# The first load of v: its second half as copies of 80, 44 and 4 rows

## The chip, the core and the metric

The kernel runs on one core of a Trainium2 chip. The time is the device time of one execution in microseconds (us); three executions before the change give the median used here. The profile is of one further execution, whose own time is told beside its span. The core has a matrix engine (PE, whose weight loads are shown as PEld), a vector engine (DVE), a scalar engine (ACT), GpSimd (POOL) and SyncE (SP), and 16 DMA engines that move data between HBM and the on-chip memory. Copies issued by SP go through the DMA queue that the profile calls q1, those issued by POOL through q0; POOL's can convert float32 to bfloat16 on the way.

## What is computed

Attention weights times values, for 8 batches and 12 heads:

```python
batch, n_heads, seq, head_dim = 8, 12, 1024, 64
np.einsum('bhqs,bhsd->bhqd', attn_weights, v).astype(np.float32)
```

`attn_weights` is float32 of 8 x 12 x 1024 x 1024 (403 MB), `v` and the result are float32 of 8 x 12 x 1024 x 64 (25 MB each).

## The kernel before, in words

**Tiling.** Four heads form a group q; there are 24 groups. Each of the 128 partitions holds 32 query rows of one head of the group. A group is worked on in two units of 16 rows each, so there are 48 units n. One load (`load_attn`, L316 to L322, issued by POOL) brings a unit into `abf[n % 2]`: 64 KB of float32 per partition, written as 32 KB of bfloat16. Two such buffers exist. The loads of the last two units are cut in halves.

**A unit.** PE transposes the 16 rows g of `abf` in groups of four matmuls (`transpose_g`, L127 to L140) into four banks; from g = 4 on, a group waits until the bank's earlier content has been copied out (L129). The copies into `at` are shared (`copy_g`, L254): DVE has ten of the sixteen rows (`on_dve`, L73), ACT six. In the first unit of each group PE also spreads v over the partitions (`spread_v`, L142) from `vr`, and DVE and ACT copy the result to `vbf`. Then PE transposes the last unit's output back (L156), multiplies (L169), and DVE and ACT copy the products to `ot`.

**v.** One load of v serves two groups (eight heads); `vr` has dimensions for the two. From the second load on, POOL loads v with conversion straight into `vr` (`load_v`, L324). The first load takes another way: SP copies it as float32 into `v32` (L383 to L387), which lies in two slots of the output buffer `osb` that are not used until late, and DVE casts it into `vr` (L308, L309). Per partition either half of v32 is 8 KB.

**Order.** Each engine has its own list of instructions, written out by hand, with semaphores between them. SP's list begins with the copies of v0, a release of output slots (L388) and a wait for the constants (L389), and goes on with one wait per load, which it passes on to PE (L390 to L410). DVE's begins with four memsets, the wait for v0 (L308) and the cast (L309); its copies of unit 0 come behind these. POOL's begins with loads 0 and 1, builds the constants, and then issues load n + 2 as soon as PE has done the transposes of unit n (L371, L372), with the loads of v and the stores of the output between them. The stores of the last eight groups are held back to the end.

**Fifteen little copies** (L397 to L402) are issued by SP beside unit 33. The k-th copies k + 1 elements of each of k partitions of the identity matrix; nothing reads them.

```python
        nc.vector.wait_ge(s_v0, 16 * 3)
        nc.vector.tensor_copy(out=vr.rearrange("p two b x -> p (two b x)"), in_=v32).then_inc(s_vr, 2)
        ...
        for two, p0, pn in ((0, 0, 16), (0, 16, P - 16), (1, 0, P)):
            nc.sync.dma_start(
                out=v32_2[ds(p0, pn), two], in_=v_2[0][ds(p0, pn), two]
            ).then_inc(s_v0, 16)
```

Of the kernel before, what the change touches and what calls it, by code (L numbers as in the profile page):

```python
# [10 lines left out]
def kernel(  # L11
# [18 lines left out]
    nc = tc.nc  # L30
# [7 lines left out]
    P = 128  # L38
# [44 lines left out]
    with tc.tile_critical(no_gpsimd_drain=True):  # L83
# [21 lines left out]
        s_v0, s_v = sem("s_v0"), sem("s_v")  # L105
# [199 lines left out]

        for h in range(2):
            nc.vector.memset(ot[:, :, ds(h * HP, HP)], 0.0).then_inc(s_ot[h])
        nc.vector.wait_ge(s_v0, 16 * 3)  # L308
        nc.vector.tensor_copy(out=vr.rearrange("p two b x -> p (two b x)"), in_=v32).then_inc(s_vr, 2)  # L309
        engine(True)  # L310
        engine(False)
# [69 lines left out]


        v32_2 = v32.rearrange("p (two x) -> p two x", two=2)  # L383
        for two, p0, pn in ((0, 0, 16), (0, 16, P - 16), (1, 0, P)):
            nc.sync.dma_start(
                out=v32_2[ds(p0, pn), two], in_=v_2[0][ds(p0, pn), two]
            ).then_inc(s_v0, 16)  # L387
# [68 lines left out]
```

## Time and profile before

| | |
|---|---|
| three executions | 1058.11, 1054.57, 1057.73 us |
| median | 1057.73 us |
| profiled execution, its own time | 1054.64 us |
| its span, first to last instruction | 1052.8 us |
| busy share of PE, DVE, ACT, POOL | 70%, 37%, 38%, 4% |
| copies of v0 by SP: 128 KB, 896 KB, 1024 KB | landed 2.9, 5.3, 26.5 us after issue |
| loads of a unit, median from issue to landing | 33.4 us |
| load 0 waited for by PE until | 28.21 us |
| v0 waited for by DVE until | 28.43 us |

Times inside the profiled execution are counted from the span's start. "Busy" of an engine leaves out its waits. In the profile's list of copies, the size is that of the written side, so a unit's load shows as 4096 KB though 8 MB are read. A line of the timeline gives start, duration, engine, source line, operation, destination and source, the number of instructions merged, and in brackets how long the engine had been idle and what ended that. A line of the DMA queues gives packets, megabytes, and the time the packets took as a share of the 16 engines' time. Besides the pages, the trace has a record of each packet's queue, start, duration and written size, and the times at which a copy's semaphore rose.

### The profile page before, as it was taken

How to read it: one execution, taken by the hardware profiler on the slowest of the kernel's cores; microseconds unless marked ns; L12 is line 12 of the kernel's file. 1: busy time of each engine (PE TensorE's matmuls, PEld its weight loads, DVE VectorE, ACT ScalarE, POOL GpSimd, SP SyncE). 2: the span in 40 equal slices, each digit the busy share in tenths (PEclk: the TensorE clock that was granted, in tenths of full speed). 3: DMA queues.
4: the chain of work that ended last, by engine and by line, in shares of the span. 5: the costliest groups of instructions: out<-in, count | busy, mean ns of one | idle time of the engine just before them, and what ended most of it. 6: DMA issues, size and time to landing. Idle time of an engine off the chain costs nothing.

```text
span 1052.8 us, 16298 instructions
## 1 busy us (share of the span) xinstructions
PE 734.0 (70%) x6920; PEld 688.6 (65%) x6920; DVE 388.4 (37%) x582; ACT 397.7 (38%) x485; POOL 45.0 (4%) x80
## 2 busy tenths in 40 slices
PE   0787687676687667667768667775666865975885
PEld 0776586566687567656668557765666865865875
DVE  0443344333353234333335324433333433532543
ACT  0443344433353334333335324433333533533543
POOL 1000000000000000000000000000000000000000
PEclk9989888898798888889879878888987987988998
DMA  9999999999999999999999999999999999999998
GB/s 234 223 218 218 205 256 219 219 216 248 229 214 256 210 218 258 219 219 230 242 218 209 258 218 219 259 218 218 249 214 219 217 212 227 219 206 226 210 215 341
DMA packets 14569, 240.21 MB, mean 228 GB/s; under 512 B 1506, under 2 KB 2018, under 8 KB 4962
## 3 DMA queue, kind: packets, MB, share of 16 engines
q0 software_dynamic: 12912, 233.84, 99.0%
q1 hardware_dynamic: 1650, 6.30, 1.6%
q8 instruction: 2, 0.03, 0.0%
q14 instruction: 5, 0.04, 0.0%
HBM read 427.82 MB, written 25.17 MB: 430 GB/s over the span
## 4 chain that ended last, share of the span: by engine, by line
DMA 78%; PE 21%; issue 1%; POOL 0%; DVE 0%; ACT 0%; POOLq 0%; SPq 0%
DMA abf<-in_attn_weights_dram 78%; PE bank L132 20%; PE bank L174 0%; PE bank L159 0%; POOL abf L319 0%; DVE osb L239 0%; ACT ot L268 0%; POOLq L451 0%; SPq L396 0%; SPq L83 0%
## 5 line engine op out<-in xcount | busy, mean ns | idle before, releaser
L132 PE MATMUL bank<-ident,abf 128*128 128x128 f32 x3072 | 450.1, 317 | 277.2 <-DMA abf<-in_attn_weights_dram 273.3
L132 PEld LDWEIGHTS bank<-ident,abf 128*128 128x128 f32 x3072 | 440.6, 214 | 290.1 <-DMA abf<-in_attn_weights_dram 285.4
L256 DVE COPY at<-bank 128x1024 bf16<-128x1024 bf16 x480 | 320.0, 689 | 468.4 <-PE bank L132 464.2
L256 ACT COPY at<-bank 128x1024 bf16<-128x1024 bf16 x288 | 288.7, 1012 | 430.2 <-PE bank L132 430.2
L174 PE MATMUL bank<-at,vbf 128*64 128x256 bf16 x3072 | 215.0, 278 | 0.0
L174 PEld LDWEIGHTS bank<-at,vbf 128*64 128x64 bf16 x3072 | 196.8, 108 | 13.4 <-DVE at L256 4.0
L268 ACT COPY ot<-bank 128x512 f32<-128x512 f32 x48 | 28.1, 586 | 181.0 <-PE bank L174 181.0
L268 DVE COPY ot<-bank 128x512 f32<-128x512 f32 x48 | 33.2, 692 | 151.4 <-PE bank L174 151.4
L159 PE MATMUL bank<-ident,ot 128*128 128x128 f32 x392 | 52.2, 276 | 32.9 <-DVE vbf L232 32.2
L159 PEld LDWEIGHTS bank<-ident,ot 128*128 128x128 f32 x392 | 43.4, 141 | 45.0 <-DVE vbf L232 44.0
L239 ACT COPY osb<-bank 128x512 f32<-128x512 f32 x97 | 52.2, 589 | 22.5 <-PE bank L159 22.5
L319 POOL DMA_DIRECT2D abf<-in_attn_weights_dram x50 | 27.2, 545 | 690.8 <-PE bank L132 689.8
L232 DVE CAST vbf<-bank 128x512 bf16<-128x512 f32 x48 | 30.9, 686 | 6.5 <-PE bank L147 6.5
L232 ACT CAST vbf<-bank 128x512 bf16<-128x512 f32 x48 | 25.8, 589 | 11.8 <-PE bank L147 11.8
L147 PE MATMUL bank<-vr,spread 32*128 32x512 bf16 x384 | 25.8, 377 | 0.0
L325 POOL DMA_DIRECT2D vr<-in_v_dram x11 | 7.7, 703 | 238.1 <-PE bank L147 238.1
L147 PEld LDWEIGHTS bank<-vr,spread 32*128 32x128 bf16 x384 | 10.1, 92 | 6.8
L309 DVE CAST vr<-osb 128x4096 bf16<-128x4096 f32 x1 | 2.3, 2294 | 25.9 <-DMA osb<-in_v_dram 25.9
L332 POOL DMA_DIRECT2D out_dram<-osb x10 | 7.1, 715 | 28.6 <-ACT osb L239 28.6
L256 ACT ACT_TABLE_LOAD x4 | 5.1, 1283 | 1.1 <-SPq L83 1.1
L356 POOL TENSOR_SCALAR_AFFINE_SELECT spread<-spread 32x512 bf16<-32x512 bf16 x4 | 2.5, 628 | 0.6
L239 DVE COPY osb<-bank 128x512 f32<-128x512 f32 x1 | 0.7, 692 | 3.1 <-PE bank L159 3.1
(8 smaller groups left out, 2.1 us busy)
## 6 DMA issues: line engine op xcount, KB each, us to landing
abf<-in_attn_weights_dram POOLq DMA_DIRECT2D x46, 4096.0 KB, 33.4
out_dram<-osb POOLq DMA_DIRECT2D x10, 2048.0 KB, 29.5
vr<-in_v_dram POOLq DMA_DIRECT2D x11, 1024.0 KB, 17.4
abf<-in_attn_weights_dram POOLq DMA_DIRECT2D x4, 2048.0 KB, 24.2
out_dram<-osb SPq DMA_DIRECT2D x1, 2048.0 KB, 13.6
osb<-in_v_dram SPq DMA_DIRECT2D x1, 1024.0 KB, 26.5
out_dram<-osb SPq DMA_DIRECT2D x1, 1024.0 KB, 15.8
osb<-in_v_dram SPq DMA_DIRECT2D x1, 896.0 KB, 5.3
```

The costliest lines, as they stand in the source:

```text
L132: last = pe.matmul(out=pt[g % 4][:, k], lhsT=words[:, k], rhs=ident, is_transpose=True, start=(k == 0), stop=(k == KW - 1),)
L147: last = pe.matmul(out=ps, lhsT=spread[rows, b], rhs=vr[rows, two, b], start=(b == 0), stop=(b == VB - 1),)
L159: last = pe.matmul(out=ps[:, ds(j * P, P)], lhsT=ot[:, j0 + j], rhs=ident, is_transpose=True, start=(j == 0), stop=(j == jn - 1),)
L174: last = pe.matmul(out=outs, lhsT=vbf[:, 2 * kw + par, h], rhs=at[:, ds(half * GH, GH), kw, ds(h * VP, VP), par], start=(n == 0), stop=(n ...
L232: copy(out=vbf[:, :, h], in_=ps.rearrange("p (k d) -> p k d", k=SB)).then_inc(s_vbf[e])
L239: return copy(out=rows.rearrange("p (half j) d -> p j half d", half=2)[:, ds(j0, jn)], in_=ps[:, ds(0, jn * P)].rearrange("p (j half d) -> ...
L256: ins = copy(out=at[:, g].rearrange("c k j two -> c (k j two)"), in_=bank[g % 4].bitcast(bf16),)
L268: copy(out=ot.rearrange("c j (h p) -> c h j p", h=VH)[:, ds(2 * e, 2)], in_=po[e].rearrange("c (h j p) -> c h j p", h=2, j=GH),).then_inc( ...
L319: pool.dma_start(out=abf[n % 2][:, ds(g0, gn)].rearrange("p g s -> p (g s)"), in_=attn_q[n // 2][:, ds((n % 2 * G + g0) * S, gn * S)],).th ...
L325: pool.dma_start(out=vr.rearrange("p two b x -> p two (b x)"), in_=v_2[iv]).then_inc(s_v, 16)
L332: eng.dma_start(out=out_2[q // 2] if fours == 2 else out_q[q], in_=at_slot if fours == 2 else at_slot[:, 0], **({"single_packet": True} if ...
L356: pool.affine_select(out=spread[ds(h * VP, VP)], in_=spread[ds(h * VP, VP)], compare_op=mybir.AluOpType.not_equal, fill=1.0, base=0, patte ...
```

## The change

The second half of v0 is no longer one copy of 128 partitions but three, of 80, 44 and 4 partitions, issued one behind the other by SP on the same queue and to the same places. Each adds 16 to the same semaphore when it has landed, so that DVE's wait before the cast goes from 3 x 16 to 5 x 16. The first half keeps its copies of 16 and 112 partitions. No other engine's list changes; SP's has two instructions more.

```diff
-        nc.vector.wait_ge(s_v0, 16 * 3)
+        nc.vector.wait_ge(s_v0, 16 * 5)
         nc.vector.tensor_copy(out=vr.rearrange("p two b x -> p (two b x)"), in_=v32).then_inc(s_vr, 2)
...
-        for two, p0, pn in ((0, 0, 16), (0, 16, P - 16), (1, 0, P)):
+        for two, p0, pn in ((0, 0, 16), (0, 16, P - 16), (1, 0, 80), (1, 80, 44), (1, 124, 4)):
             nc.sync.dma_start(
                 out=v32_2[ds(p0, pn), two], in_=v_2[0][ds(p0, pn), two]
             ).then_inc(s_v0, 16)
```

## The prediction

> **What bounds the kernel now.** I read the page's totals first, then the chain that ended last, then the timeline of the first 60 us, and last the DMA view of one short window.
>
> ```profile
> span 1052.8 us, 16298 instructions
> DMA  9999999999999999999999999999999999999998
> q0 software_dynamic: 12912, 233.84, 99.0%
> q1 hardware_dynamic: 1650, 6.30, 1.6%
> HBM read 427.82 MB, written 25.17 MB: 430 GB/s over the span
> DMA abf<-in_attn_weights_dram 78%; PE bank L132 20%; PE bank L174 0%; PE bank L159 0%; POOL abf L319 0%; DVE osb L239 0%; ACT ot L268 0%; POOLq L451 0%; SPq L396 0%; SPq L83 0%
> osb<-in_v_dram SPq DMA_DIRECT2D x1, 1024.0 KB, 26.5
> ```
>
> The 16 DMA engines are at 9 in every slice but the last, and every other engine waits for them. So the end comes when the last DMA engine is through its bytes; what makes a DMA engine idle, or gives the last one more to do, costs its full length, and what PE, DVE or ACT do counts only if it delays the issue of a load. The last line quoted is the copy that is changed: the second half of v0 needs 26.5 us to land, the 896 KB copy ahead of it 5.3.
>
> ```profile
> 0.96 1.32 SPq L385 DMA_DIRECT2D osb<-in_v_dram  x3
> 1.48 1.24 POOL L319 DMA_DIRECT2D abf<-in_attn_weights_dram  x2 [1.04 <-SPq L83]
> 28.21 9.96 PE L132 MATMUL bank<-ident,abf 128*128 128x128 f32 x64 [28.21 <-DMA abf<-in_attn_weights_dram]
> 28.43 2.29 DVE L309 CAST vr<-osb 128x4096 bf16<-128x4096 f32 x1 [25.86 <-DMA osb<-in_v_dram]
> 30.64 1.28 DVE L256 COPY at<-bank 128x1024 bf16<-128x1024 bf16 x2
> 38.47 0.57 POOL L319 DMA_DIRECT2D abf<-in_attn_weights_dram  x1 [32.25 <-PE bank L132]
> 48.55 9.48 PE L132 MATMUL bank<-ident,abf 128*128 128x128 f32 x64 [2.54 <-DMA abf<-in_attn_weights_dram]
> ```
>
> DVE stands at the cast of v0 (L309) until 28.43, and its copies of unit 0 are queued behind it. They free the banks for PE's transposes; when all 64 are done, POOL issues load 2, at 38.47. At that time the DMA engines still work on load 1. By the packet records 15 of them begin load 2 at 46.96 to 47.16 with no gap. Load 2 was thus issued 8.5 us ahead of its first packet: that is the cover for any delay of DVE.
>
> Why the half takes 26.5 us, the DMA view of 6 to 28 us shows:
>
> ```profile
> q0 software_dynamic: 144, 4.19, 88.4%
> q1 hardware_dynamic: 144, 1.05, 11.8%
> ```
>
> 144 packets of either queue, nine each per engine: SP's queue and POOL's take turns, one packet for one. Per engine q1 has eight rows of 8 KB and one completion packet, q0 eight rows of load 0 (2.41 us each alone) and its completion. A load packet with a v row behind it takes 2.73 us (starts at 5.78, 8.51, 11.24), and 5.78 + 8 x 2.73 = 27.6 is where the half ends.
>
> **The change part by part.** *Instructions.* SP issues five copies in place of three, 0.44 us each (1.32 / 3): the last is issued 0.9 us later, at about 3.2 us, before its turn comes; nothing there. Behind them on SP are a release and the wait for the constants (done at about 6.2), used only at 28: nothing. DVE's wait rises from 48 to 80: the same cast, later. PE, ACT, POOL and DVE keep their instructions.
>
> *Turns.* A copy's completion packet takes a turn of its own: in the packet records around 800 us each of the 15 little copies of L400 shows one data packet and then, one load packet (2.43 us) later, its 4-byte packet. On the busiest engine 80 rows are 5 rows and a completion. 44 rows are 4 and a completion if they are split evenly on 11 engines, and 3 and one if unevenly on 16. 4 rows are 1 and one, if these too start at the first engine. So 13 turns (12 at least) against 9 before. I take 13: the copies of this queue seen so far are split evenly (1, 7 and 8 rows per engine), and no more than 11 of 16 engines can share 44 evenly. If it were split on four engines, it would be 20.
>
> *Arrival of v0.* One turn falls on load 0's completion, the other 12 behind load packets, ten with a row: 5.78 + 12 x 2.41 + 10 x 0.32 = 37.9. The same count gives 27.6 for before. From the completion packet to the start of the cast took 0.7 to 0.8 (27.6-27.8 to 28.43): the cast starts at 38.6 in place of 28.43, its end moves from 30.72 to 40.9.
>
> *Unit 0.* Load 0 lands as before, near 28; PE transposes four of the 16 groups and then needs a bank that DVE empties: the first copy ends at about 41.5. Twelve groups, 48 transposes, are left. In unit 0 of before, after a long idle time, the first 21 started 0.213 us apart and the others 0.121. PE has again been idle for 10 us, so 21 x 0.213 + 27 x 0.121 = 7.7, end at 49.3; without the slow start 5.8, end at 47.3. I take the slow start, as its row is the same operation after idle. POOL follows 0.3 later (38.17 to 38.47): load 2 is issued at 49.6 (47.6 to 49.6) in place of 38.47.
>
> *The DMA queue.* The cover of 8.5 us is gone: the engines run out of load 1 at 46.0 to 47.6 and stand still. What they lose depends on the time from POOL's issue to the first packet, which no row shows for an idle queue in mid-run. From below: SP's first copy, issued at 0.96, moved its first packet at 1.98, so 1.0. From above: load 0, issued at 1.48, moved its first packet at 5.78, 4.3, with SP's rows in front of it. No case in between shows it (the v load issued at 80.07 moved at 85.61, behind a full queue, so 5.5 is an outer bound). I take 3.4: nearest is the same instruction's own start, less the first use: the completion of SP's first copy took up to 1.2 us to land, later ones 0.5. Load 2 then starts at 53.0 in place of 47.0: **6.0 us lost**. Ends: 47.6 + 1.0 gives 1.6 lost, 49.6 + 5.5 gives 8.1.
>
> The Trainium skill, "DMA: Bandwidth & Descriptors", section "Latency and other measured facts", states about 1 us to the first byte for such a load; the sum by it would be 3.6 lost, an estimate. No run here shows it.
>
> *Balance.* Two engines land last in every load (992.56 and 992.63, the others from 990.64 to 991.45). Each met one 16 KB packet of instructions, at 44.67 and at 59.19; in L400's copies they first appear at the copies of 12 and of 13 rows, so they are among those that get three rows fewer, 3 x 0.32 = 0.96 us. This would be the gain. But a stall that lets all 16 engines run dry starts them together on load 2 and wipes it out, and PE's delay puts both instruction packets (44.67 + 11 and 59.19 + 9) behind the restart, so the same two are late again. Worth 0.
>
> *Afterwards.* Unit 0 ends 11 us later, at 57.1 (46.0 before); unit 1's transposes take 9.5, load 3 is issued at 66.9, and load 2 leaves the engines 8 x 2.41 = 19.3 after 49.6 + 3.4. Both share the 3.4, so the margin is 49.6 + 19.3 - 66.9 = 2.0 us: no second stall. From then on the loads set the pace as before.
>
> *Sum.* The profiled execution took 1054.64 (span 1052.8 and 1.8 around it): 1060.6. It lies 3.1 below the median of the runs shown, 1057.73, which lie in two places (1054.57; 1057.73, 1058.11). What separates them the profile does not tell; two of three were high, so I add to the median: 1057.73 + 6.0 = **1063.7**.
>
> **The rivals.** *No stall (not slower).* The place is SP's queue between 6 and 38 us. If the rows of one copy, or its completion, did not take turns of their own, v0 would not be late. It decides at 8.5 us less the start time: with 3.4, a cast up to 5 us late costs nothing, that is up to two more turns of 2.41. Then the balance counts: the two late engines gain 0.96, but others, 0.8 ahead of them, get one or two rows more (0.32 or 0.64), so 0.4 to 0.8 is left of it: 1054.64 - 0.6 = 1054.0 by the profiled execution, 1057.1 by the median. For it: nothing shows several hardware copies in turn with a large load at the start. Against it: 144 to 144. The Trainium skill, same page, section "Queues, rings and completion order", says that an engine changes queues after a whole packet, typically 9 to 17 descriptors; by that each of the three new copies would need one turn and this rival would be right. The trace disagrees so far, 144 to 144, each row by itself.
>
> *More turns.* Load 0's first packet came at 5.78, just behind the last row of the 896 KB copy. If it comes 1 us sooner, two rows and a completion wait for turns too, and then the three copies; or 44 rows lie on fewer engines. Every turn costs 2.41 straight, now that the cover is gone: 1 to 4 turns are 1066 to 1073. For it: such a start would give the higher runs of before. Against it: nothing in the one execution shown varies.
>
> *Second stall.* If PE stays slow in unit 1 (one stretch of before, 50 to 55 us, ran at a granted clock of 0.66), load 3 misses its 2.0 us: 1 to 2 more, 1065 to 1066.
>
> **How the numbers follow.** One stall 62 in 100, no stall 12, more turns 18, second stall 8. A measurement here can't tell less than about 0.5% from no change: 1052.4 to 1063.0. One stall (1.6 to 8.1 lost) lies above that in 38 of its 62, within in 24; more turns and second stall lie above; no stall within, or in 2 of its 12 below. Slower 0.64, same 0.34, faster 0.02. The range, 1056.5 to 1070, takes in the stall's ends and most of the added turns, and leaves out the low half of no stall and the longest turns, 17 in 100.
>
> **What would show it.** The cast of L309 near 38.6; PE's first transposes in two pieces, some 16 by 32 and the rest after 41; POOL's third load near 49.6; a hole in the DMA share between 47 and 53, and none later; periods of 43.5 us after it as before. Wrong: the cast before 34, or DMA engines busy through 47 to 53.

## The result

The changed kernel took 1061.53 us in the median of six executions (1060.29 to 1061.67), the kernel before 1054.82 (1054.44 to 1058.11). The ratio of their times is 1.0051, with a 95% interval of 1.0036 to 1.0067: slower by half a per cent. (It lies below the ratio of the two medians because two of the six executions before were 3 us above the rest; the means give 1.0051.) The profiled execution took 1060.29 us against 1054.64, so 5.65 us are to be found in the trace.

The page of the changed kernel, its totals and queues:

```profile
span 1058.5 us, 16300 instructions
...
DMA  9899999999999999999999999999999999999998
...
q0 software_dynamic: 12912, 233.84, 98.6%
q1 hardware_dynamic: 1665, 6.30, 1.6%
...
HBM read 427.82 MB, written 25.17 MB: 428 GB/s over the span
```

The bytes are the same and q1 has 15 packets more: 11 + 4 completions, as will be seen below. The only slice that lost a tenth is the second, 26 to 53 us. The chain of work that ended last, for the first 75 us:

```profile
2.79 36.44 DMA osb<-in_v_dram
...
39.33 0.07 DVE vr L309
...
41.54 0.69 DVE at L256
...
42.28 7.35 PE bank L132 x48
...
57.48 7.96 PE bank L132 x64
...
65.73 26.61 DMA abf<-in_attn_weights_dram
```

Before the change this chain was in a load up to 48.51; now it runs through the copies of v0, the cast, DVE's first copy and PE's remaining 48 transposes of unit 0. The timeline has the same steps:

```profile
0.96 2.19 SPq L385 DMA_DIRECT2D osb<-in_v_dram  x5
...
29.00 3.31 PE L132 MATMUL bank<-ident,abf 128*128 128x128 f32 x16 [29.00 <-DMA abf<-in_attn_weights_dram]
...
39.33 2.29 DVE L309 CAST vr<-osb 128x4096 bf16<-128x4096 f32 x1 [36.76 <-DMA osb<-in_v_dram]
...
42.28 7.35 PE L132 MATMUL bank<-ident,abf 128*128 128x128 f32 x48 [9.96 <-DVE at L256]
...
49.93 0.58 POOL L319 DMA_DIRECT2D abf<-in_attn_weights_dram  x1 [43.71 <-PE bank L132]
```

Load 2 is issued at 49.93 in place of 38.47. The table by stretches (busy time of each engine, then PE's granted clock, the DMA share and GB/s) shows what the DMA engines did meanwhile. First the kernel before, then the changed one:

```profile
46.40:48.60 2.20, 0.04 (x1) 0.05 (x1) 0.00 (x0) 0.24 (x1) 0.00 (x0) 1.00 1.11 238
48.60:51.20 2.60, 2.60 (x17) 2.60 (x18) 1.38 (x2) 1.01 (x1) 0.00 (x0) 0.76 0.94 202
```

```profile
46.40:48.60 2.20, 2.20 (x20) 2.20 (x20) 1.76 (x4) 1.84 (x2) 0.00 (x0) 1.00 0.01 0
48.60:51.20 2.60, 2.03 (x25) 1.25 (x23) 2.16 (x4) 1.66 (x4) 0.58 (x1) 1.00 0.00 0
```

The share counts packets by their start, so the packets of load 1 that began at 45.4 to 46.2 still run until 48.6 on eleven engines. From 48.6 to 51.2 nothing moves on any. The first packet of load 2 starts at 51.20; before, at 46.96.

The 5.65 us are made up as follows. 4.24 are the later first packet (51.20 - 46.96). 0.6 are the first packets themselves: the first row of load 2 took 2.75 to 3.43 us on the 16 engines, where a row takes 2.43. Load 2 is 4.80 later on its first engine (66.61 to 71.41). 0.8 come at 151 us, where the last row of load 6 (counted from 0) took 2.8 to 3.5 us on all 16 engines (before, only three took over 2.5 in that place, 2.56 to 2.78): from there on, load after load lands 5.6 later, to the end.

How v0 came to be late is in the DMA view of 6.3 to 39 us:

```profile
q0 software_dynamic: 208, 6.29, 90.0%
q1 hardware_dynamic: 159, 1.05, 8.3%
```

159 packets of q1 are 80 + 44 + 4 rows and 16 + 11 + 4 completions: the 44 rows went to 11 engines, four each. The 208 of q0 are 13 per engine. By the packet records the busiest engines took their rows at 8.4 to 19.9, a completion at 22.1, four rows at 24.5 to 31.4, a completion at 33.5, a row at 35.9 and the last completion at 38.7 to 38.9: thirteen turns, each behind a packet of q0.

### The profile page after: what moved, and what is told of

Same layout as the page of the kernel before. It is cut to its first block, busy times and chain, and to the rows that moved or that the text cites. A ratio compares the mean times of both kernels' runs of the same rounds, so it can differ in the third digit from the quotient of the medians.

```text
span 1058.5 us, 16300 instructions
## 1 busy us (share of the span) xinstructions
PE 730.7 (69%) x6920; PEld 685.1 (65%) x6920; DVE 388.1 (37%) x582; ACT 397.6 (38%) x485; POOL 45.0 (4%) x80
## 4 chain that ended last, share of the span: by engine, by line
DMA 76%; PE 21%; issue 1%; DVE 0%; SPq 0%; ACT 0%; POOL 0%; DVEq 0%
DMA abf<-in_attn_weights_dram 73%; PE bank L132 20%; DMA osb<-in_v_dram 3%; PE bank L174 1%; PE bank L159 0%; SPq L385 0%; DVE vbf L232 0%; PE bank L147 0%; DVE at L256 0%; DVE osb L239 0%; ACT ot L268 0%; POOL abf L319 0%; DVEq L255 0%; DVE vr L309 0%; DVEq L289 0%
```

## The experiments

The theory: every row and every completion in SP's queue waits for one packet of a load (a turn), the last turn sets the cast, the cast sets PE and so the issue of load 2, and each us by which that comes too late is a us of idle DMA engines. The rivals: the bytes per engine have become uneven; or the additional copies have a price of their own. All ratios are to the kernel before, run beside. Wherever the number of copies changes, DVE's wait counts them all; where the code cut doesn't show that line, it is part of the edit all the same.

### Even bytes, thirteen turns

```diff
+        for k in range(2):
+            nc.sync.dma_start(
+                out=small[:, 1, k, 0:4], in_=v_2[0][0:16, 1, 0:4]
+            ).then_inc(s_v0, 16)
-        nc.vector.wait_ge(s_v0, 16 * 3)
+        nc.vector.wait_ge(s_v0, 16 * 5)
```

> Nothing of the computation is left out; two copies of 16 rows of 16 bytes, which nothing reads, go behind the even second half, and DVE's wait counts them. Bytes of v0 stay even, eight rows per engine; turns go from 9 to 13, as in the changed kernel. Turns theory (each row and each completion waits for one packet of the load): one turn falls on load 0's completion, so the last completion comes at about 6.0 + 12 x 2.41 + 8 x 0.32 = 37.5, the cast of L309 starts near 38.2, load 2 is issued near 48.8 (10.6 after the cast, as in the changed kernel), its first packet comes 1.3 later; DMA engines stand still about 3 us, and with 0.6 more for the slow first packets 3.7 to 4.5 us are lost: 1058.5 to 1059.5. Rival, uneven bytes per engine cost the time: the bytes are even here, so 1054.8, no change, and the cast near 28.5 to 31.

Measured: 1060.61 us against 1055.04, ratio 1.0056 (1.0040 to 1.0071): the whole loss of the change, with even bytes and half a kilobyte of extra data. The timeline:

```profile
38.15 2.29 DVE L309 CAST vr<-osb 128x4096 bf16<-128x4096 f32 x1 [35.58 <-DMA small<-in_v_dram]
...
41.09 8.50 PE L132 MATMUL bank<-ident,abf 128*128 128x128 f32 x48 [8.97 <-DVE at L256]
...
49.90 0.57 POOL L319 DMA_DIRECT2D abf<-in_attn_weights_dram  x1 [43.69 <-PE bank L132]
```

The cast is where the count of turns put it, 38.15 for 38.2, held by a copy of 16 times 16 bytes. By the packet records even these small packets waited one by one: the rows of 16 bytes at 30.2 to 30.5 and 35.1 to 35.3, their completions at 32.7 to 32.9 and 37.5 to 37.7. The issue is 1.1 later than expected, since PE's 48 transposes took 8.50, not 7.35. Uneven bytes are not needed for the loss.

### Four even copies, twelve turns

```diff
-        for two, p0, pn in ((0, 0, 16), (0, 16, P - 16), (1, 0, P)):
+        for two, p0, pn in ((0, 0, 16), (0, 16, P - 16), (1, 0, 32), (1, 32, 32), (1, 64, 32), (1, 96, 32)):
```

> Nothing is left out; the second half goes as four even copies of 32 rows: still eight rows per engine, 12 turns. Turns theory: last completion at 6.0 + 11 x 2.41 + 8 x 0.32 = 35.1, cast near 35.8, load 2 issued near 46.4, first packet 47.7, when the engines have been out of load 1 since 47.0: 0.7 to 1.4 us lost, 1055.5 to 1056.2; this is the edge of the cover. Rival, the number of SP's copies costs the time (two more cost 5.7): three more, 1060 or more. Rival, uneven bytes: 1054.8.

Measured: 1058.02 against 1055.04, ratio 1.0027 (1.0016 to 1.0038), and the profiled execution 1057.44.

```profile
36.17 2.29 DVE L309 CAST vr<-osb 128x4096 bf16<-128x4096 f32 x1 [33.60 <-DMA osb<-in_v_dram]
...
46.71 0.57 POOL L319 DMA_DIRECT2D abf<-in_attn_weights_dram  x1 [40.49 <-PE bank L132]
```

Cast and issue are within 0.4 of the count (35.8 and 46.4), and so at the edge of the cover. The loss is 1.6 to 2.3 us more than expected; load 2 lands 1.56 later on its first engine, of which the late issue explains 1.0 (first packet at 47.99), and 1.05 more come at the last row of load 6. Four copies cost half of what three cost: the number of copies does not set the price.

### Three copies of 80, 32 and 16 rows, eleven turns

```diff
-        for two, p0, pn in ((0, 0, 16), (0, 16, P - 16), (1, 0, P)):
+        for two, p0, pn in ((0, 0, 16), (0, 16, P - 16), (1, 0, 80), (1, 80, 32), (1, 112, 16)):
```

> Nothing is left out; the second half goes as three copies, as in the changed kernel, but of 80, 32 and 16 rows: five, two and one row per engine, eight in all, even; 11 turns. Turns theory: last completion at 6.1 + 10 x 2.41 + 8 x 0.32 = 32.8, cast near 33.5, load 2 issued near 44.1 and moving at 45.4, before the engines run out at 47.0: no loss, 1055.0, and no standstill. Rival, three copies in place of one cost the time: 1060 to 1061.

Measured: 1056.39 against 1055.12, ratio 1.0009 (0.9999 to 1.0019); the ten executions spread from 1054.94 to 1058.73, and the profiled one was the slowest. The interval includes no change. In the profiled execution the cast started at 34.26, PE's 48 transposes took 8.45, and load 2 was issued at 45.96. Its first packet could come at 47.2, when the first engines had just run dry (load 1 ends at 47.2 to 48.3 in that execution), so eleven turns are on the edge, where I had expected no standstill. The edge explains only part of this execution, though: of the first rows of load 2 on the 16 engines, seven began at 47.37 to 47.59, the other nine only at 48.51 to 50.33, although the last packet of load 1 was at 48.29. What held those nine was not found, and why the executions spread is not shown. Still, three copies cost a fifth of what the change costs, so it is not their number.

### Eight even copies, sixteen turns

```diff
-        for two, p0, pn in ((0, 0, 16), (0, 16, P - 16), (1, 0, P)):
+        for two, p0, pn in ((0, 0, 16), (0, 16, P - 16), *((1, p, 16) for p in range(0, P, 16))):
```

> Nothing is left out; the second half goes as eight even copies of 16 rows: eight rows per engine, 16 turns. Turns theory, with the times measured so far: last completion at 6.1 + 15 x 2.41 + 8 x 0.32 = 44.8, cast near 45.4, load 2 issued near 56.0 and moving at 57.3, 10.3 after the engines ran out; with 0.6 for the slow first packets and 0.8 to 1.0 for the later slow ones 11.7 to 11.9 lost: about 1066.8. Rival, uneven bytes: 1055.0, as the bytes are even. Rival, each additional copy costs a fixed time (2 to 3 us by the changed kernel, 1 by the four copies of 32): 7 to 20 us, from 1062 up, but with the cast not where the turns put it.

Measured: 1070.33 against 1055.12, ratio 1.0143 (1.0126 to 1.0160).

```profile
48.33 2.29 DVE L309 CAST vr<-osb 128x4096 bf16<-128x4096 f32 x1 [45.75 <-DMA osb<-in_v_dram]
...
51.27 8.45 PE L132 MATMUL bank<-ident,abf 128*128 128x128 f32 x48 [18.13 <-DVE at L256]
...
60.02 0.57 POOL L319 DMA_DIRECT2D abf<-in_attn_weights_dram  x1 [53.80 <-PE bank L132]
```

This is 3.5 above the expectation; load 2 was issued 4.0 later than expected, at 60.02 for 56.0. 2.9 of the 4.0 are the cast. One engine had its first load packet before the last row of the first half, one turn more for it (127 rows of v0 were under way before the first load packet, not 128): its last completion was at 47.87, the latest of the others at 46.67, so this explains 1.2. Another 1.0, in the mean of the engines, is that 69 rows of loads 0 and 1 took 2.5 to 2.9 us in place of 2.43, for a reason that the trace does not tell; the remaining 0.7 was not followed. 1.1 of the 4.0 are PE's slower transposes. Against the kernel with the two tiny copies, which has thirteen turns, load 2 is issued 10.1 later and the kernel is 9.7 slower: past the edge the price is one for one.

### Uneven bytes, but nobody waits

This edit is to the changed kernel; `s_v1` is a new semaphore.

```diff
-        nc.vector.wait_ge(s_v0, 16 * 5)
-        nc.vector.tensor_copy(out=vr.rearrange("p two b x -> p (two b x)"), in_=v32).then_inc(s_vr, 2)
+        nc.vector.wait_ge(s_v0, 16 * 2)
+        nc.vector.tensor_copy(
+            out=vr[:, 0].rearrange("p b x -> p (b x)"), in_=v32[:, 0 : SB * D * VB]
+        ).then_inc(s_vr)
...
             load_attn(n + 2)
+            if n == 0:
+                pool.wait_ge(s_v1, 16 * 3)
+                pool.tensor_copy(
+                    out=vr[:, 1].rearrange("p b x -> p (b x)"), in_=v32[:, SB * D * VB : 2 * SB * D * VB]
+                ).then_inc(s_vr)
...
-            ).then_inc(s_v0, 16)
+            ).then_inc(s_v1 if two else s_v0, 16)
```

> Nothing is left out; copies of 80, 44 and 4 rows as in the changed kernel, but DVE casts the first half of v0 alone, as soon as that has landed (near 7 us), and POOL casts the second half after it has issued load 2; the second half has a semaphore of its own. Turns theory: the late half is waited for by nobody who matters, PE is not held up, load 2 is issued near 38, the DMA engines never run dry: 1054.0 to 1054.8, and the two late engines land 0.5 to 1.0 closer to the others than before. Rival, the uneven bytes or the copies themselves cost the time: 1060 to 1061 as in the changed kernel.

Measured: 1055.76 against 1055.04, ratio 1.0005 (0.9996 to 1.0014). With the copies of 80, 44 and 4 rows in place the loss is gone:

```profile
7.04 1.23 DVE L310 CAST vr<-osb 128x2048 bf16<-128x2048 f32 x1 [4.47 <-DMA osb<-in_v_dram]
...
28.97 9.92 PE L133 MATMUL bank<-ident,abf 128*128 128x128 f32 x64 [28.97 <-DMA abf<-in_attn_weights_dram]
...
39.19 0.57 POOL L322 DMA_DIRECT2D abf<-in_attn_weights_dram  x1 [32.99 <-PE bank L133]
...
39.81 1.89 POOL L378 CAST vr<-osb 128x2048 bf16<-128x2048 f32 x1
```

DVE is free at 8.3, PE does all 64 transposes in one piece, and load 2 goes out at 39.19. The copies themselves, and the uneven bytes, cost nothing that shows. The expected gain did not come either; the next run says why.

### Split cast with the even copy

The same kernel with `(1, 0, P)` and `s_v1` waited for to 16.

> Nothing is left out; the same split cast, with the even copy of 128 rows. Turns theory: 1054.8 as before, within 0.3; two late engines about 1.9 behind the first as before. Against the split cast with 80, 44 and 4 rows it gives the worth of the balance alone, 0 to 0.8 us. If the wait for v0 cost something even before the change, this is faster than before by that.

Measured: 1055.68 against 1055.04, ratio 1.0004 (0.9995 to 1.0013). Against the run above this gives the worth of the balance alone: 0.08 us, none. In the semaphore records load 2 lands between 66.81 and 68.19 here and between 66.01 and 68.49 with the uneven copies: the relieved engines are 0.8 earlier, but the last one is 0.3 later. The rows that were taken from the late engines made others the last. That the kernel is not faster than before shows as well that the wait for v0 cost nothing then.

### Two of the three copies on ACT's queue

```diff
-        for two, p0, pn in ((0, 0, 16), (0, 16, P - 16), (1, 0, P)):
+        for two, p0, pn in ((0, 0, 16), (0, 16, P - 16), (1, 0, 80)):
...
         engine(True)
+        v32_a = v32.rearrange("p (two x) -> p two x", two=2)
+        for p0, pn in ((80, 44), (124, 4)):
+            nc.scalar.dma_start(out=v32_a[ds(p0, pn), 1], in_=v_2[0][ds(p0, pn), 1]).then_inc(s_v0, 16)
         engine(False)
```

> Nothing is left out; copies of 80, 44 and 4 rows as in the changed kernel and the same wait for all of them, but the last two are issued by ACT, on a queue of its own. Turns theory: turns are counted per queue, so no queue has more than 7 turns for the second half, or about 11 if rows of the first half are still on the way when load 0 begins: cast between 24 and 33.5, load 2 moving before 47.0, no loss: 1055.0 to 1055.7. Rival, uneven bytes or the number of copies: 1060 to 1061.

Measured: 1057.36 against 1055.12, ratio 1.0021 (1.0012 to 1.0031); the profiled execution was an outlier of its own with 1063.37. It missed, and does not decide whether turns are counted per queue. What the profile of that execution shows is something else: ACT's 48 rows went first, and only 48 of SP's 128 rows of the first half were under way when load 0 began; the other 80 then took turns, with 80 of the second half. The cast came at 41.61. The turns were moved, not saved.

### Load 2 late, v0 untouched

```diff
+            if n == 0:
+                pool.wait_ge(s_abf[1], 16)
             load_attn(n + 2)
```

> Nothing is left out; the copies of v0, the cast and everything on PE, DVE, ACT and SP are as before the change; POOL alone waits, ahead of load 2, until load 1 has landed whole (near 48.5). Load 2 is then issued near 48.6 and moves 1.3 later, at 49.9, in place of 47.0. Theory, the late issue of load 2 is the whole price: 2.9 lost and 0.6 for slow first packets, 1058.6; if the slow packets at the end of load 5 belong to the restart and not to v0's copies, 0.8 to 1.0 more, 1059.5. Rival, part of the price lies in v0's copies or in PE's pause: less than 2.9 lost, and the cast, at 28.4, says it is not v0.

Measured: 1060.54 against 1055.35, ratio 1.0050 (1.0033 to 1.0067).

```profile
29.13 9.97 PE L132 MATMUL bank<-ident,abf 128*128 128x128 f32 x64 [29.13 <-DMA abf<-in_attn_weights_dram]
...
29.34 2.29 DVE L309 CAST vr<-osb 128x4096 bf16<-128x4096 f32 x1 [26.77 <-DMA osb<-in_v_dram]
...
49.93 0.58 POOL L319 DMA_DIRECT2D abf<-in_attn_weights_dram  x1 [43.71 <-DMA abf<-in_attn_weights_dram]
```

POOL's wait let load 2 go 1.3 later than I had reckoned, at 49.93, which happens to be the time in the changed kernel. Here v0 and PE's transposes are as before the change, and the ratio is that of the change, 1.0050 to 1.0051. The first rows of load 2 took 2.6 to 3.5 us here too, and the last row of load 6, at 151 (the expectation calls it load 5), was again slow on all 16 engines. So the late issue of load 2 is the whole price, and both after-effects belong to the restart of idle DMA engines.

## Why the prediction was right, point by point

**What bounds the kernel**: as said. A DMA standstill of 4.24 us in the second slice is found again at the end, with 1.4 more of its after-effects.

**Turns and arrival of v0**: thirteen turns, five, four and one row with a completion each, as counted; the 44 rows on 11 engines. The last completion was due at 37.9 and came at 38.7 to 38.9: load 0 began 0.2 to 0.3 later (6.00 to 6.25), and some packets around 28 took longer. The cast came at 39.33 for 38.6. What the Trainium skill says on the choice of the number of engines, the largest number up to 16 that divides the partitions ("DMA: Bandwidth & Descriptors", "Why a DMA increments its semaphore by 16 and not by 1"), agrees with the 11 completions of the 44 rows. The rule of the Trainium skill on whole packets of 9 to 17 descriptors (same page, "Queues, rings and completion order"), which the prediction cited for the rival without a stall, doesn't hold for these copies: each row and each completion waited by itself.

**Unit 0**: the 48 transposes took 7.35 for 7.7, and load 2 was issued at 49.93 for 49.6. PE's slow start after the idle time was part of it: without it the issue would have come some 1.5 earlier. It is seen in PE's granted clock in the changed kernel, which the prediction did not use (a line of the table by stretches, from just before the two shown above):

```profile
40.00:46.40 6.40, 4.12 (x23) 4.12 (x24) 4.81 (x6) 1.01 (x1) 0.00 (x0) 0.58 1.02 220
```

The 0.58 is the mean of 0.50, which the trace records until 45.40, and 1.00 behind it; at 45.3 to 45.5 the transposes go over from 0.213 us apart to 0.121. 14 of the 48 were slow here, 26 or 27 in the runs in which they took 8.45 to 8.50. In unit 0 of before the profile shows a clock of 1.00, but its records of the clock begin only at 32.88, just where the spacing changes.

**The DMA queue**: the term that was mis-sized. From POOL's issue to the first packet I took 3.4 us, nearest to load 0's own start; it measured 1.27 (49.93 to 51.20), and 1.26 to 1.29 in five of the experiments. (Nor does the working there give 3.4: 4.3 less the difference of 1.2 and 0.5 is 3.6.) The lower bound, from SP's first copy, was the right row. The roughly 1 us to the first byte that the Trainium skill states ("DMA: Bandwidth & Descriptors", "Latency and other measured facts"), which I set aside, is nearly met. The stall itself was 4.24 in place of 6.0. The total is near the forecast, 5.65 for 6.0, because two costs were not in the sum: 0.6 for the first rows and 0.8 for the last rows of load 6. That is luck: 1.8 too much and 1.4 too little nearly cancel.

**Balance**: right in the sum, at 0. The instruction packets came at 57.07 and 66.73, both after the restart, and two engines are again 1.0 later than the rest when load 2 lands (72.97 and 72.98, the others to 71.94). Wrong in the rival: 0.4 to 0.8 was to be left of the gain without a stall, and with the split cast nothing is: the uneven copies are 0.08 slower. I had compared with the engines' distances at the end of the run, 0.8; near load 2 the other engines lay within 0.2 of one another, so two rows more made the last.

**Afterwards**: no second stall, as reckoned; load 3 was issued at 65.73 for 66.9.

**Base**: I added to a median of 1057.73. Of six executions before, four lie at 1054.4 to 1054.8, and of those beside the experiments 48 of 51 at 1054.8 to 1055.7; so the sum against the profiled execution, 1060.6, was closer to 1061.53 than 1063.7 was. The spread of the first three was not a property of the kernel to be carried over.

## What to carry to other kernels

A small copy that runs beside a large load is not timed by its bytes but by its packets in its queue: count rows and completions on the busiest engine and multiply by the duration of one packet of the load (here 2.41 us, and 0.32 for a row of 8 KB); splitting it, even evenly, adds a turn per copy. Then follow who waits for it and compare with the lead that the next load's issue has: inside the lead the delay is free, past it each us costs a us when the DMA engines are the bound. And a small rebalancing of bytes over the engines was worth, in the one comparison made here, only the distance from the last to the next, at the place where it acts.

## What the runs showed that I had not expected

A load issued by POOL to an idle queue moved its first packet after 1.26 to 1.29 us in six kernels; the 4.3 us at the start of the program are no measure of it.

After a standstill of the engines the first row of a load took 2.5 to 3.6 us on the 16 engines in place of 2.43, and in every kernel whose engines had stood still the last row of load 6, about 100 us later and the last before the first store, took 2.7 to 4.1 on nearly all of them; in the kernels without a standstill at most three engines did, 2.56 to 2.78. What ties these rows to the restart was not found: the load after it, and the same place in later groups, are as before.

The moment at which load 0's first packet comes, 5.8 to 6.1 us, falls just behind the last row of v0's first half. In some kernels one to five engines began with the load a row earlier (123 to 127 of 128 rows under way); each such engine has a turn more. This is the mechanism of the rival with more turns; in the eight copies it is seen to delay the cast by 1.2, and it is argued, not shown, to be why the executions of the three even copies spread over 4 us.
